# Cumulative sums of a decoder layer's state-space heads stored by head, so that a decay row is read in one piece

## The chip, the cores and the metric

The kernel runs on one core of one Trainium2 chip. What is measured is the device time of one execution in microseconds (us), from the first to the last instruction and what the runtime puts around them. Five engines work beside each other, each through its own instructions in order: TensorE (PE in the profile, its weight loads PEld), VectorE (DVE), ScalarE (ACT), GpSimd (POOL) and SyncE (SP), which only issues transfers. Transfers (DMAs) run on 16 engines of their own and are issued here from SP, ACT and POOL.

## What is computed

One decoder layer on 512 tokens of width 1024, in float32: a SwiGLU feed-forward part, a mixer, cross-attention to 256 memory tokens, a second feed-forward part and a norm. The mixer has two groups of heads that share an input and an output projection: eight differential-attention heads and 16 Mamba-2 (SSD) heads of width 64, in four groups. The change concerns the SSD heads. They work in chunks of 128 tokens:

```python
la_cum = jnp.cumsum(la, axis=2)                     # la = dt * a, per chunk and head
seg = la_cum[:, :, :, None] - la_cum[:, :, None, :]
decay = jnp.exp(jnp.where(causal[None, None, :, :, None, None], seg, -jnp.inf))
cb = jnp.einsum('bclgn,bcsgn->bclsg', cc, bc)
y_diag = jnp.einsum('bclsg,bclsgr,bcsgrp->bclgrp', cb, decay, xdt)
y_off = jnp.einsum('bclgn,bcgrpn,bclgr->bclgrp', cc, prev, jnp.exp(la_cum))
```

So each head needs, for its four chunks, the differences of the cumulative sums of all pairs of tokens in a chunk. For that, every partition (token s) needs the head's sums of all 512 tokens l in its row, and its own sum as a bias.

## The kernel before

**Precision and weights.** Most products are made of float32 split in two parts (`split_into`, L155 and L156: ACT rounds to the high part, DVE subtracts for the low part) and three matmuls. Weights come as 512 KB tiles `wr` by SP (`load_w`, L174; `raw_w`, L246) into six buffers, and are split into `wh` (ACT) and `wl` (DVE) before PE can use them. So behind each weight tile stand one ACT and one DVE instruction, in the order of those engines' streams.

**Order.** The work is written as generators. Dense ones (projections) run in a list; chains (attention heads, SSD groups, sums) are spawned with a due time and are taken between steps of the dense ones by a modelled PE clock. SP and POOL run in the order of the code; PE, DVE and ACT are put in order by the framework's scheduler. What each instruction waits for are semaphores; transfers of SP and ACT share eight of them (the lanes) in turn, so a transfer can't be issued until the previous one on its lane has landed.

**The cumulative sums.** After the `dt` projection (`steps_dense`, `pdt`), the chain `steps` makes `la` (128 tokens of a chunk on the partitions, chunk x head = 4 x 16 columns), and a matmul with a triangle of ones gives `cum` [128, 4, 16], at the time when the dense work is the attention's values (`by_token`, L356, with tiles `va`, `ve`, `vb`). `cum` is transposed on PE (`pct`, 64 rows = chunk x head, 128 tokens), copied by DVE to `ct_sb` (L727) and stored by POOL to `cum_d` in DRAM (L728), one row of 512 B for each chunk and head, chunks outermost.

**The decay rows.** `decays(g, j)` issues, on ACT's queue (L900), for two heads hd the load of the head's sums into all 128 partitions: 4 chunks x 128 tokens, 2 KB a partition, 256 KB in all. In `cum_d` a head's four chunks lie 16 rows apart, so that a partition's 2 KB come in four pieces of 512 B. The rows land in the tiles `gate` (j = 0) and `th` (j = 1), which the feed-forward parts use at other times. There are 16 such loads: four right behind the store, and four for each next group g + 1, issued in `group(g)`, two behind each of its two sets of `py` matmuls, when the tile is free again. ACT then makes of them the exponentials `e` (L964), the differences (L966) and the decays (L967), and DVE multiplies with `cbm` (L968).

**Others on the same queue.** The attention heads load their bias rows on ACT's queue too (`bias`, L757: 128 partitions x 2 KB, one piece each, eight times), for the softmax whose minimum `mn` DVE makes (L778). POOL and SP also copy and add up weight blocks in DRAM (`isum`, `wsum`, L1227 and L1231) for the last feed-forward part.

Of the kernel before, what the change touches and what calls it, by code (L numbers as in the profile page):

```python
# [11 lines left out]
F32 = mybir.dt.float32  # L12
# [5 lines left out]
P = 128  # L18
T = 512
# [81 lines left out]
def body(tc, a, dbg=None):  # L101
    nc = tc.nc
# [8 lines left out]
    dram = ctx.enter_context(tc.tile_pool(name="dram", bufs=1, space=bass.MemoryType.DRAM))  # L111
# [3 lines left out]
    def nm(s):  # L115
        uid[0] += 1
        return f"{s}_{uid[0]}"

    def s2(s, dt=F32, shape=(P, T)):
        if math.prod(shape[1:]) <= T // 2:  # L120
            return sp.tile(list(shape), dt, tag="s1", name=nm(s), bufs=NHALF)
        return sp.tile(list(shape), dt, tag="s2", name=nm(s))

    def s4(s):
        return sp.tile([P, 4, T // 2], F32, tag=s, name=nm(s), bufs=1)

    def small(s, n, bufs=None):
        return tiny.tile([P, n], F32, tag=s, name=nm(s), bufs=bufs)
# [4 lines left out]
    def aux(s, shape=(P, T)):  # L133
        return aux_p.tile(list(shape), F32, tag="aux", name=nm(s))

    def dump(name, t):
        if dbg and name in dbg:
            nc.sync.dma_start(dbg[name], t.bitcast(F32) if t.dtype == R32 else t)

    last, start, last_sum, recent, newest, newest_mm = [], [], [], [], [], []  # L140
    V, S, G = nc.vector, nc.scalar, nc.gpsimd
    od = Order()

    def mm(out, w, x, start, stop):
        od.t += (1 if w.dtype == R32 else 4) * (x.free_size() + 8) / 2400
        newest_mm[:] = [nc.tensor.matmul(out, w, x, start=start, stop=stop).ins]  # L146

    def transpose(out, x):
        od.t += 2 * (P + 8) / 2400
        nc.tensor.transpose(out, x, ident)  # L150
# [161 lines left out]
    def by_token(blocks, g, ps, done):  # L312
# [30 lines left out]
        kept = []  # L343
        w = weights("m1", 0)
        for i, (name, out, which, part) in enumerate(steps):
            (wh, wl), first = w, name in ("m1", "t")
            if i + 1 < len(steps):
                w = weights(steps[i + 1][0], steps[i + 1][3])
# [176 lines left out]
    def block_tiles(g, n):  # L525
        def steps(th, blocks, apart):
            b11 = [s2("g11" + p_, R32, (P, H)) for p_ in "hl"]
            split_into(*b11, th[:, 0])
            blocks["11"] = tuple(b11)
            yield apart  # L530
            for sums in sums_in_steps(*(th[:, i] for i in range(4)), pair=(th[:, 0:2], th[:, 1:3])):
                blocks |= sums or {}
                yield apart
            raw = split("g", th[:, 2:4].rearrange("p a b -> p (a b)"))
            lo, hi = slice(0, H), slice(H, T)
            blocks |= {"22": hl(raw, lo), "12": hl(raw, hi)}

        def made(th):
            g.append({})
            if len(g) < n:  # L540
                od.spawn(steps(th, g[-1], 2.9), 2.9)
            else:
                for _ in steps(th, g[-1], 0.0):
                    pass
        return made
# [52 lines left out]
    st_mix, h, h_sums = Stat(), [], []  # L598
# [59 lines left out]
    def bc_c(t):  # L658
        return t[:, None, :].to_broadcast([P, 4, 16])

    def flat(t):
        return t.rearrange("p a b -> p (a b)")

    def col64(s):
        return cp.tile([P, 4, 16], F32, name=s)

    cum, cdec, dend, dth = col64("cum"), col64("cdec"), col64("dend"), col64("dth")
    cum_d = dram.tile([64, P], F32, name="cum_d")

    def steps_dense():  # L670
        wdt = s2("wdt", shape=(P, KT, 16))
# [11 lines left out]
    def steps(pdt):  # L683
        dtf = s2("dtf", shape=(32, T))
        S.activation(dtf, pdt, AF.Copy)
        ii = s2("ii", shape=(32, 16))
        nc.gpsimd.dma_start(ii, a["ii"])
        hb = s2("hb", shape=(P, 2, 16))
        nc.gpsimd.dma_start(hb, a["hb"].partition_broadcast(P))
        yield 4.5  # L690
        pdk = aux("pdk", (P, 4, 16))
        for c in range(4):
            mm(pdk[:, c, :], dtf[:, c * P : (c + 1) * P], ii, True, True)
        dtr, dta, dtz, dte, dtp, la = (s2("dt", shape=(P, 4, 16)) for _ in range(6))
        V.tensor_tensor(dtr, pdk, bc_c(hb[:, 0]), ALU.add)

        S.activation(dta, dtr, AF.Abs)
        S.activation(dte, dta, AF.Exp, scale=-1.0)
        V.tensor_scalar(dtz, dte, 2.0, None, ALU.add)
        V.reciprocal(dtz, dtz)  # L700
        V.tensor_tensor(dtz, dtz, dte, ALU.mult)
        V.tensor_tensor(dte, dtz, dtz, ALU.mult)
        V.tensor_scalar(dtp, dte, 1.0 / 19, None, ALU.mult)
        for n in range(17, 2, -2):
            V.scalar_tensor_tensor(dtp, dtp, 1.0 / n, dte, ALU.add, ALU.mult)
        V.scalar_tensor_tensor(dtp, dtp, 1.0, dtz, ALU.add, ALU.mult)
        V.tensor_scalar(dtr, dtr, 0.0, None, ALU.max)
        V.scalar_tensor_tensor(dtr, dtp, 2.0, dtr, ALU.mult, ALU.add)
        dump("dt", dtr)
        ea = small("ea", 16, bufs=1)  # L710
        G.tensor_tensor(ea, euler[:, 0:1].to_broadcast([P, 16]), hb[:, 1], ALU.pow)
        V.scalar_tensor_tensor(la, dtr, -1.0, bc_c(ea), ALU.mult, ALU.mult)
        V.tensor_scalar(dth, dtr, 0.5, None, ALU.mult)
        yield 7.5
        pcum = aux("pcum", (P, 2, 64))
        mm(pcum[:, 0], tri, flat(la), True, True)
        mm(pcum[:, 1], ones, flat(la), True, True)
        V.tensor_copy(flat(cum), pcum[:, 0])
        V.tensor_tensor(flat(dend), pcum[:, 1], flat(cum), ALU.subtract)
        S.activation(flat(cdec), pcum[:, 1], AF.Exp)  # L720
        S.activation(dend, dend, AF.Exp)
        V.tensor_scalar(dend, dend, 0.5, None, ALU.mult)
        yield 1.5
        pct = aux("pct", (64, P))
        transpose(pct, flat(cum))
        ct_sb = s2("ct_sb", shape=(64, P))
        V.tensor_copy(ct_sb, pct)  # L727
        nc.gpsimd.dma_start(cum_d, ct_sb)  # L728
        for j in range(2):
            decays(0, j)  # L730
        dump("cum", cum)
# [162 lines left out]
    def decays(g, j):  # L894

        rows_of[g, j], both = [], s4(("gate", "th")[j])
        for hh in range(2):
            r = both[:, 2 * hh : 2 * hh + 2].rearrange("p a (b c) -> p (a b) c", c=P)
            hd = 4 * g + 2 * j + hh
            S.dma_start(r, bass.AP(cum_d.tensor, cum_d.offset + hd * P, [[0, P], [16 * P, 4], [1, P]]))  # L900
            rows_of[g, j].append(r)

    def group(g, bt, ct, xs, zs):
# [52 lines left out]
        for j in range(2):  # L956
# [21 lines left out]
            if g < 3:  # L978
                decays(g + 1, j)
# [497 lines left out]
```

## Time and profile before

| | |
|---|---|
| median of 3 runs | 1360.78 us (1359.14 to 1363.01) |
| profiled execution, its span | 1365.5 us (4.7 above the median; no other time of it is recorded) |
| PE busy | 1313.2 us, 96% |
| DVE, ACT, POOL busy | 998.0 (73%), 676.1 (50%), 117.2 (9%) |
| mean granted clock of TensorE | 0.982 |
| row loads (L900) | 16, of 256 KB each |
| first and last of them issued | at 432.7 and 799.7 us |

In the timeline a line gives start and duration in us, the engine (a q behind it: only the engine's sequencer is at work, as in issuing a transfer), line, operation, out<-in, how many, and in brackets the idle time of the engine before it and what ended it. In the list of waits a line gives who waited for whom, the sum in us, how often, and the longest. In a table by stage a line gives a stretch and its length, the busy time of PE, PEld, DVE, ACT and POOL with the number of instructions, the granted clock (1.00 is full), the busy share of the DMA engines and GB/s. Of one line's or tile's instructions the view gives the smallest, median and largest duration in ns, the first and last start, and the time from issue to landing. Names carry no buffer numbers, and a helper's line stands for all its callers.

### The profile page before, as it was taken

The page shows a single profiled execution, that of the slowest core. Times are in us where ns is not written, and L with a number is a line of the kernel's source. Part 1 is how long each engine was busy: PE and PEld are TensorE (multiplying, and loading weights), DVE is VectorE, ACT ScalarE, POOL GpSimd, SP SyncE. Part 2 cuts the span into 40 slices and gives each one's busy share as a digit, 9 for nine tenths or more (in the row PEclk, how much of TensorE's full clock was granted, in tenths as well). Part 3 has the DMA queues.
Part 4 walks back from the last instruction along what each step waited for, and adds up shares of the span by engine and source line. Part 5 has one row for each costly group of instructions (what it writes and reads, how often), then busy time and mean ns, then how long its engine had stood idle before and what let it go on. Part 6 is the DMA issues. An engine that isn't in the chain of part 4 may idle for free. (4 is left out here: it accounts for less than half of the span.)

```text
span 1365.5 us, 20091 instructions
## 1 busy us (share of the span) xinstructions
PE 1313.2 (96%) x7745; PEld 1138.7 (83%) x7745; DVE 998.0 (73%) x1565; ACT 676.1 (50%) x1134; POOL 117.2 (9%) x131
## 2 busy tenths in 40 slices
PE   9999999999977899998999998999999999999997
PEld 7898998899865577875788886888889989989995
DVE  6875778578885577656777777655587888977896
ACT  6441544245443466434646446434455555554564
POOL 0000011000010001110110220210001000000001
PEclk9999999999999899999999999999999999999998
DMA  7435586474464833665357747858057866666662
GB/s 264 123 109 131 147 207 220 105 199 142 141 163 123 243 106 78 156 184 165 74 125 208 176 111 252 246 161 223 33 155 180 233 211 187 178 194 183 181 205 93
DMA packets 75007, 225.85 MB, mean 165 GB/s; under 512 B 8520, under 2 KB 20272, under 8 KB 74560
## 3 DMA queue, kind: packets, MB, share of 16 engines
q1 hardware_dynamic: 52688, 175.47, 38.4%
q0 software_dynamic: 12480, 42.55, 17.4%
q10 hardware_dynamic: 9744, 6.56, 2.5%
q8 instruction: 61, 1.00, 0.3%
q14 instruction: 34, 0.28, 0.1%
HBM read 222.39 MB, written 50.91 MB: 200 GB/s over the span
## 5 line engine op out<-in xcount | busy, mean ns | idle before, releaser
L155 ACT ACTIVATE wh<-wr 128x1024 fp32r<-128x1024 f32 (+2 forms) x317 | 322.9, 1021 | 374.8 <-PE po L146 61.7
L156 DVE TENSOR_TENSOR wl<-wr,wh 128x1024 fp32r<-128x1024 f32 (+2 forms) x317 | 372.3, 1177 | 115.8 <-ACT wh L155 113.1
L146 PE MATMUL po<-gh,wh 128*128 128x512 f32 x176 | 68.8, 392 | 0.0
L146 PE MATMUL po<-gl,wh 128*128 128x512 f32 x176 | 68.5, 390 | 0.0
L146 PE MATMUL po<-gh,wl 128*128 128x512 f32 x176 | 68.4, 389 | 0.0
L240 PE MATMUL qa<-hmh,wl 128*128 128x256 f32 x216 | 61.2, 283 | 0.1
L240 PE MATMUL qa<-hml,wh 128*128 128x256 f32 x216 | 61.1, 283 | 0.0
L240 PE MATMUL qa<-hmh,wh 128*128 128x256 f32 x216 | 61.1, 283 | 0.0
L779 ACT ACTIVATE ec<-ec,mn 128x512 f32<-128x512 f32 (+3 forms) x64 | 35.5, 556 | 38.2 <-DVE mn L778 38.2
L146 PE MATMUL pxbc<-hnh,wh 128*128 128x512 f32 x128 | 52.3, 408 | 0.0
L146 PE MATMUL pxbc<-hnl,wh 128*128 128x512 f32 x128 | 50.3, 393 | 0.0
L146 PE MATMUL pxbc<-hnh,wl 128*128 128x512 f32 x128 | 50.2, 392 | 0.0
L584 DVE TENSOR_TENSOR upd<-po,row 128x512 f32<-128x512 f32 x24 | 16.6, 691 | 39.0 <-PE po L146 38.8
L240 PE MATMUL qb<-s31h,wh 128*128 128x256 f32 x152 | 43.2, 284 | 0.8 <-ACT u L299 0.8
L240 PE MATMUL qe<-s31h,wl 128*128 128x256 f32 x152 | 43.2, 284 | 0.5 <-DVE wl L156 0.5
L240 PE MATMUL qb<-s24h,wl 128*128 128x256 f32 x152 | 43.1, 284 | 0.5 <-DVE wl L156 0.5
L240 PE MATMUL qe<-s31h,wh 128*128 128x256 f32 x152 | 43.1, 283 | 0.2 <-DVE nlam L635 0.2
L240 PE MATMUL qb<-s24h,wh 128*128 128x256 f32 x152 | 43.0, 283 | 0.0
L240 PE MATMUL qe<-s24h,wh 128*128 128x256 f32 x152 | 43.0, 283 | 0.0
L240 PE MATMUL qb<-s31h,wl 128*128 128x256 f32 x152 | 43.0, 283 | 0.0
L240 PE MATMUL qe<-s24h,wl 128*128 128x256 f32 x152 | 43.0, 283 | 0.0
L240 PE MATMUL qb<-hmh,wh 128*128 128x256 f32 x152 | 43.0, 283 | 0.0
(490 smaller groups left out, 4105.0 us busy)
## 6 DMA issues: line engine op xcount, KB each, us to landing
wr<-in_f2q SPq DMA_DIRECT2D x44, 512.0 KB, 4.4
wr<-in_f1q SPq DMA_DIRECT2D x40, 512.0 KB, 4.3
isum<-in_f2q SPq DMA_DIRECT2D x22, 512.0 KB, 6.1
wr<-isum SPq DMA_DIRECT2D x22, 512.0 KB, 4.2
wsum<-in_f2b SPq DMA_DIRECT2D x20, 512.0 KB, 7.6
wr<-wsum SPq DMA_DIRECT2D x20, 512.0 KB, 4.4
wr<-in_f1q POOLq DMA_DIRECT2D x16, 512.0 KB, 5.8
wr<-in_f1o SPq DMA_DIRECT2D x16, 512.0 KB, 4.5
```

The source lines that it names most:

```text
L146: newest_mm[:] = [nc.tensor.matmul(out, w, x, start=start, stop=stop).ins]
L155: S.activation(hi, src, AF.Copy),
L156: V.tensor_tensor(lo, src, hi.bitcast(F32), ALU.subtract),
L240: newest_mm[:] = [nc.tensor.matmul(out, a_[:, wc], b_, start=first and f == 0 and kp == 0 and j == 0, stop=kp == n - 1 and j == 2, skip_gr ...
L584: V.tensor_tensor(upd, po, row4, ALU.mult)
L779: S.activation(ec[:, :n], ec[:, :n], AF.Exp, bias=mn, scale=-1.0, accum_out=sm[c][:, i : i + 1])
```

## The change

The sums are stored with the heads outermost: `cum_d` becomes [16, 512], a row of 2 KB for each head with its four chunks behind each other. The transpose must then give its 64 rows in the order head x chunk, so DVE first copies `cum` [token, chunk, head] to a new tile `ct_h` [token, head, chunk], and PE transposes that. The store writes the same 32 KB, from 64 partitions. A load reads one row of `cum_d`, broadcast to 128 partitions: the same 2 KB a partition, in one piece.

```diff
-    cum_d = dram.tile([64, P], F32, name="cum_d")
+    cum_d = dram.tile([16, T], F32, name="cum_d")
...
         pct = aux("pct", (64, P))
-        transpose(pct, flat(cum))
+        ct_h = s2("ct_h", shape=(P, 16, 4))
+        V.tensor_copy(ct_h, cum.rearrange("p c h -> p h c"))
+        transpose(pct, flat(ct_h))
         ct_sb = s2("ct_sb", shape=(64, P))
         V.tensor_copy(ct_sb, pct)
-        nc.gpsimd.dma_start(cum_d, ct_sb)
+        nc.gpsimd.dma_start(cum_d.rearrange("h (c t) -> (h c) t", t=P), ct_sb)
...
-            hd = 4 * g + 2 * j + hh
-            S.dma_start(r, bass.AP(cum_d.tensor, cum_d.offset + hd * P, [[0, P], [16 * P, 4], [1, P]]))
+            S.dma_start(r.rearrange("p a b -> p (a b)"), cum_d[4 * g + 2 * j + hh : 4 * g + 2 * j + hh + 1].to_broadcast([P, T]))
```

Lines behind L728 move down by two, and those from L901 on by one (L900 becomes L901). On DVE, where the sums are made, there stood (the numbers in the names are the buffers'):

```order
L718 COPY cum<-pcum_4243 128x64
L719 TENSOR_TENSOR dend<-pcum_4243,cum 128x64
L156 TENSOR_TENSOR wl_4288<-wr_4137,wh_4287 128x1024
L722 TENSOR_SCALAR dend<-dend 128x64
L727 COPY ct_sb_4263<-pct_4261 64x128
```

and now stand

```order
L718 COPY cum<-pcum_4243 128x64
L719 TENSOR_TENSOR dend<-pcum_4243,cum 128x64
L726 COPY ct_h_4262<-cum 128x64
L156 TENSOR_TENSOR wl_4290<-wr_4137,wh_4289 128x1024
L722 TENSOR_SCALAR dend<-dend 128x64
L729 COPY ct_sb_4265<-pct_4261 64x128
```

One copy has come in ahead of a weight split; the rest of DVE's order is the same to the end. On PE, at the same place, the transpose `pct` among the value matmuls stood before as

```order
L356 MATMUL vb_4098<-wh_4230,s24l_3981 128x512
L356 MATMUL vb_4098<-wl_4231,s24h_3980 128x512
L150 MATMUL pct_4261<-ident,cum 64x128
L356 MATMUL vb_4098<-wh_4230,s24h_4025 128x512
L356 MATMUL vb_4098<-wh_4230,s24l_4026 128x512
L356 MATMUL vb_4098<-wl_4231,s24h_4025 128x512
```

and stands now as

```order
L356 MATMUL vb_4098<-wh_4230,s24l_3981 128x512
L356 MATMUL vb_4098<-wl_4231,s24h_3980 128x512
L356 MATMUL vb_4098<-wh_4230,s24h_4025 128x512
L356 MATMUL vb_4098<-wh_4230,s24l_4026 128x512
L150 MATMUL pct_4261<-ident,ct_h_4262 64x128
L356 MATMUL vb_4098<-wl_4231,s24h_4025 128x512
```

It has moved behind two matmuls; nothing else on PE has changed place. On ACT, the four first loads and what stands behind them, before:

```order
L370 ACTIVATE u_743_4284<-vb_4099 128x512
L900 DMA gate_4266<-cum_d 128x4x128 x2
L900 DMA th_4269<-cum_d 128x4x128 x2
L155 ACTIVATE vh_4324<-p_731_4225 128x512
L155 ACTIVATE wh_4333<-wr_4112 128x1024
```

and now:

```order
L370 ACTIVATE u_744_4286<-vb_4099 128x512
L901 DMA gate_4268<-cum_d 128x512 x2
L901 DMA th_4271<-cum_d 128x512 x2
L155 ACTIVATE vh_4326<-p_731_4225 128x512
L155 ACTIVATE wh_4335<-wr_4112 128x1024
```

The order is the same, and the loads have become rows of 512 numbers. The orders of SP and POOL are unchanged.

## The prediction

> **What bounds the kernel now.** I read the page first, for the bound:
>
> ```profile
> span 1365.5 us, 20091 instructions
> PE 1313.2 (96%) x7745; PEld 1138.7 (83%) x7745; DVE 998.0 (73%) x1565; ACT 676.1 (50%) x1134; POOL 117.2 (9%) x131
> q10 hardware_dynamic: 9744, 6.56, 2.5%
> ```
>
> TensorE (PE) is busy for 96% of the span, so a change pays only where PE stands idle or runs at a lower clock. The queue that carries the decay rows, q10, takes 2.5% of the transfer engines: by volume it can't matter. By packets it is large for its 6.56 MB: 16 row loads of 128 x 4 pieces make 8192 of the 9744.
>
> Next came PE's waits over the whole run, for the places where it stands idle (us in total, times, longest):
>
> ```profile
> PE ve L356 <- ACT wh L155: 10.9, 1, 10.9
> PE ps L146 <- DVE mn L778: 7.6, 3, 5.7
> PE pdt L146 <- DVE ql L160: 7.6, 1, 7.6
> PE pm L146 <- ACT wh L155: 7.0, 2, 5.7
> PE pt L150 <- DVE mn L778: 1.6, 1, 1.6
> PE pq L146 <- ACT wh L155: 0.7, 1, 0.7
> PE pk L146 <- DVE wl L156: 0.5, 1, 0.5
> ```
>
> And the table by stage for the stretches at half clock (PE busy, PEld, DVE, ACT, POOL, then the granted clock):
>
> ```profile
> 440.20:450.30 10.10, 4.07 (x9) 2.80 (x10) 4.82 (x6) 4.59 (x6) 0.00 (x0) 0.50 0.85 131
> 474.30:481.10 6.80, 5.02 (x15) 3.95 (x16) 4.79 (x18) 4.40 (x13) 0.00 (x0) 0.50 0.61 228
> 593.80:597.10 3.30, 3.30 (x12) 2.79 (x10) 2.26 (x2) 0.55 (x1) 0.00 (x0) 0.50 0.75 187
> 624.50:631.30 6.80, 6.19 (x17) 4.62 (x17) 6.27 (x15) 4.03 (x9) 0.00 (x0) 0.50 0.60 181
> 825.90:832.60 6.70, 4.90 (x12) 3.77 (x13) 5.72 (x9) 4.84 (x9) 0.00 (x0) 0.50 0.90 264
> ```
>
> Each long wait is followed by such a stretch, in which PE's busy time counts double. The wait at pdt belongs to the projection that feeds the sums, so it is over before a row can be loaded; the others lie at the five places of this table, A to E in its order. The question is which of them the row loads cause.
>
> **Place A, the first four loads (433 to 451 us).** ScalarE (ACT) issues them itself, in order with its other work. Its timeline:
>
> ```profile
> 427.75 0.58 ACT L370 ACTIVATE u<-vb 128x512 f32<-128x512 f32 x1
> 432.71 1.10 ACTq L900 DMA_DIRECT2D gate<-cum_d  x2
> 433.85 10.66 ACTq L900 DMA_DIRECT2D th<-cum_d  x2
> 444.56 0.63 ACT L155 ACTIVATE vh<-p 128x512 fp32r<-128x512 f32 x1 [16.23 <-issue]
> 445.10 1.04 ACT L155 ACTIVATE wh<-wr 128x1024 fp32r<-128x1024 f32 x1
> ```
>
> PE's, and the store on POOL that the loads wait for:
>
> ```profile
> 446.19 0.79 PE L356 MATMUL ve<-wh,s24h 128*128 128x512 f32 x1 [10.90 <-ACT wh L155]
> 426.47 0.64 POOL L728 DMA_DIRECT2D cum_d<-ct_sb  x1 [25.92 <-DVE ct_sb L727]
> ```
>
> ACT is free at 428.3, is held until the store has landed (432.7), and is then held to 444.5 by the issues themselves, of which the second pair alone takes 10.66. Behind them in its queue stand vh and the weight split wh that PE waits for. The rows of the loads, and of the bias loads on the same queue, tell why:
>
> ```profile
> L900 ACTq DMA_DIRECT2D gate<-cum_d x8: 367/458/2368, 432.7 to 790.3; - x8
> L900 ACTq DMA_DIRECT2D th<-cum_d x8: 367/518/10101, 433.9 to 799.7; - x8
> DMA to landing us min/median/max: 7.5/11.8/29.8
> L757 ACTq DMA_DIRECT2D bias<-rel_z x8: 326/338/360, 401.1 to 664.6; - x8
> DMA to landing us min/median/max: 2.7/3.1/19.2
> ```
>
> A bias load is what a row load becomes: 128 partitions, 256 KB, one 2 KB piece each, on ACT's queue. Its issue never took over 360 ns; a row load's took up to 10101. So the 10 us go with the number of pieces: four loads put 2048 into one queue, and the fourth has to wait until it has drained. After the change the four put 512 there, as many as the first load alone does now, and the first pair (1024) is issued in 1.10.
>
> What the change adds here is one strided copy on DVE and a later transpose; the nearest row for the copy is
>
> ```profile
> 424.25 0.23 DVE L718 COPY cum<-pcum 128x64 f32<-128x64 f32 x1 [0.65 <-PE pcum L146]
> ```
>
> Queued behind it are the DVE split wl, ct_sb and the store, so the store lands some 0.23 late, at 432.9. It delays ACT by that much; for PE, matmuls at hand cover it. If that cover is gone it costs 0.2 to 0.5. Of the moved transpose (one matmul, two places later) nothing remains beside it. Four issues take 1.4 (at 338 ns) to 2.2 (at the first pair's 0.55); I take 1.7, so ACT goes on at 434.6 instead of 444.56. PE follows 1.63 behind (446.19 - 444.56), at 436.3: of the 10.9 idle 1.0 is left, a gain of 9.9. The 4.07 busy at half clock become 2.0, a gain of 2.0. Behind the first matmuls DVE's split is next late, since vl and wl follow ACT's: 0.5 back. Together 11.4.
>
> Whether the 1.5 us left idle still lowers the clock is open. The nearest row is place C, where waits of about 1.4 and 0.7 were followed by the stretch from 593.80 at 0.50, at a price of half of its 3.30. I charge half of that, 0.8: A gains 10.6. The ends: 9 with the whole lowered clock (1.6) and the slower issues, 12 without DVE's 0.5.
> The Trainium skill (TensorE: Matmul & The Clock Gate, "HAM oscillation — how this bites in real kernels") says that only idle gaps over about 3.4 us lower the clock; by that rule A would be 11.4. The trace disagrees: no gap before 593.80 was so long.
>
> **Place B (470 to 481).** SyncE (SP) shares completion lanes with ACT's queue, so its prefetch waits for the row loads to land:
>
> ```profile
> SPq L1227 <- DMA gate<-cum_d: 15.5, 1, 15.5
> 449.05 2.91 SPq L174 DMA_DIRECT2D wr<-in_wk  x1
> 468.50 1.06 ACT L155 ACTIVATE wh<-wr 128x1024 fp32r<-128x1024 f32 x1 [10.30 <-DMA wr<-in_wk]
> ```
>
> The key weights are issued right behind that wait and land only at 468.4. ACT's and DVE's splits of them hold up the softmax work behind, and PE waits at pk (0.5), ps (7.6 less the 5.7 of place D) and pt (1.6): 4.0. The 5.02 at half clock cost 2.5. The lane comes free when the first load has landed, which by the 15.5 is some 16 us after its issue now; with a quarter of the pieces I estimate 4 to 6, so the weights are issued about 10 earlier and have fewer pieces to compete with; PE, some 11 earlier, needs them at about 458 (468.5 less 10.6). Even at the old 19.4 from issue (449.05) to use they would be there at about 458. I count all 6.5; the ends are 0 and 6.5.
>
> **Places C and D (584 to 631).** The next loads, on ACT, and what waits for them:
>
> ```profile
> 584.30 2.78 ACTq L900 DMA_DIRECT2D gate<-cum_d  x2
> 587.13 1.29 ACT L964 ACTIVATE e<-th 64x512 f32<-64x512 f32 x2 [6.17 <-DVE y L992]
> 591.32 0.61 ACT L155 ACTIVATE wh<-wr 128x512 fp32r<-128x512 f32 x1
> 591.99 0.50 PE L146 MATMUL pm<-yah,wh 128*128 128x512 f32 x1 [1.36 <-ACT wh L155]
> 598.43 1.22 ACTq L900 DMA_DIRECT2D th<-cum_d  x2
> 605.00 0.34 ACTq L757 DMA_DIRECT2D bias<-rel_z  x1
> 624.35 0.69 DVE L778 CUSTOM_DVE_ANT_0 ec<-ps,bias 128x512 f32<-128x512 f32 x1 [10.15 <-DMA bias<-rel_z]
> ```
>
> C: the exponentials e (587.13) start as soon as the two issues are done, and wh (591.32) shows no idle time before it. So 2.78 becoming 0.7 brings wh 2.1 earlier and covers the 1.4. The wait at pq (0.7) and 1.7 of half clock go only if DVE's splits also come up: 3.7 at most, 0 at least, I take 2.5.
> D: the bias of the next head stands in ACT's queue behind 1024 row pieces and lands 19.2 after its issue; DVE is idle for 10.15 and PE for 5.7. With 256 pieces ahead, the 605.00 issue should land by 610, at the median 3.1 by 608, while DVE is ready only at 614. So all 5.7 go, and half of 6.19: 8.8. The lower end is 5.7.
>
> **Place E and the later loads** stay. At E, ACT waits for DVE and then has its queue full:
>
> ```profile
> 820.36 1.29 ACT L155 ACTIVATE ysh<-y 128x512 fp32r<-128x512 f32 x2 [2.69 <-DVE y L1009]
> 827.04 0.61 ACT L155 ACTIVATE wh<-wr 128x512 fp32r<-128x512 f32 x1
> ```
>
> The split that PE wants (5.7 at pm) starts 6.7 later and has no idle time before it; what ACT waited for is y, not a row load. The loads around 734 and 790 hold up no matmul; their speed is worth nothing. In the built program PE now also waits on the loads' lanes ahead of 16 py matmuls; ACT has read those rows long before, so I charge 0.4 for instructions alone.
>
> **Sum.** 10.6 + 6.5 + 2.5 + 8.8 - 0.4 = 28.0 us against the profiled span: 1365.5 - 28.0 = 1337.5. That execution is 4.7 above the median of the three runs, 1360.78, of which I take the same 28.0: **1332.8**.
>
> **Rivals.**
> 1. The key weights become what is late. They land at 468 as now, for the transfers ahead of them rather than for the lane. For: the 10.30 in the row of 468.50. Against: they were issued at 449 only because of the lane. Then PE arrives early and waits, A and B are worth nothing, C and D bring 11.3: 1349.5. Chance 0.09.
> 2. Bytes, not pieces, set the pace: the same 4 MB are read, 128 partitions from one row as before. Then ACT's issue and the landings stay: 1361.0. For: q10's median of 11.8 would fit a slow shared source. Against: bias loads of the same bytes take 3.1 and 338 ns. Chance 0.06. The Trainium skill (DMA: Bandwidth & Descriptors, "Specifications") speaks for it: it calls 512 B enough for line rate; the issue of 10101 ns is not explained by that.
> 3. Slower: SP, released early, puts its DRAM copies of 512 KB ahead of the key weights while POOL's are under way. It decides once the weights land after 480, 12 past today's 468, when C and D are used up; each further us costs one. Landing at 486 gives 1366. It needs some 45 us from issue to landing, where 19 is the worst seen at B. Chance 0.02.
>
> **How the numbers follow.** The forecast has 0.83. All terms at their upper ends (12, 6.5, 3.7, 8.8) give 31.0 and 1329.8, and the runs scatter by some 2 below: 1327. At the lower ends, with half of B (9, 3.2, 0, 5.7), 17.9 give 1342.9; 3 more for a part given back later: 1346. The rivals lie outside, with 0.17. Faster by over 0.3% (4 us, about what a measurement of this kernel can tell from none): 0.92; within: 0.06; slower: 0.02.
>
> **What would show it.** Right: row loads issued in under 0.6 us each, landing in 3 to 8; PE going on near 436 to 437; PE's waits at ve about 1, at ps and pt near nothing, and 6 us at pm left; two or three half-clock stretches fewer. Wrong: an ACT issue of several us, a bias wait of DVE near 600, a wait for in_wk, or PE waits past 860 that are not there now.

## The result and the profile after

| | before | after |
|---|---|---|
| median, us (4 runs each on one chip) | 1359.96 (1356.42 to 1363.01) | 1339.29 (1336.95 to 1341.09) |
| profiled execution, its span, us | 1365.5 | 1335.1 (timed as 1336.95) |

The ratio of the times is 0.9842 [0.9811, 0.9874]: 20.7 us faster, where 28.0 had been forecast and 1332.8 named. From profile to profile it is 30.4. The two figures differ by the two executions that were profiled. The new one is the fastest of four, 2.3 under its median. Its time is 1.8 above its span; with the same 1.8 the profiled execution before took 1367.3, 7.3 above the median of its kernel. 30.4 - 7.3 - 2.3 = 20.8.

The head of the page after, to set beside that of before:

```profile
span 1335.1 us, 20107 instructions
PE 1302.0 (98%) x7745; PEld 1131.7 (85%) x7745; DVE 997.6 (75%) x1566; ACT 676.2 (51%) x1134; POOL 116.5 (9%) x131
q10 hardware_dynamic: 3600, 6.56, 1.5%
```

The packets of q10 went from 9744 to 3600, and their time from 2.5% to 1.5%. PE's waits after the change (us in total, times, longest), of the places that the prediction speaks of:

```profile
PE pdt L146 <- DVE ql L160: 7.5, 1, 7.5
PE pm L146 <- ACT wh L155: 6.1, 2, 5.7
PE ve L356 <- ACT wh L155: 1.8, 1, 1.8
PE pq L146 <- ACT wh L155: 0.7, 1, 0.7
PE ve L356 <- DVE wl L156: 0.5, 1, 0.5
```

Gone are the 10.9 at ve, the ps, pt and pk; the 5.7 at pm (place E) and the wait at pdt stay. The table by stage after, behind place A and at place E (length, PE busy, PEld, DVE, ACT, POOL, granted clock):

```profile
436.60:446.00 9.40, 8.85 (x38) 7.03 (x39) 8.35 (x9) 6.50 (x9) 0.00 (x0) 1.00 1.06 275
795.00:801.50 6.50, 3.55 (x8) 2.70 (x9) 5.48 (x9) 5.99 (x13) 0.00 (x0) 0.50 0.37 109
```

Behind A the clock is no longer lowered at all; at E it still is. ACT at place A after:

```profile
427.36 0.58 ACT L370 ACTIVATE u<-vb 128x512 f32<-128x512 f32 x1
432.71 1.01 ACTq L901 DMA_DIRECT2D gate<-cum_d  x2
433.77 1.18 ACTq L901 DMA_DIRECT2D th<-cum_d  x2
434.99 0.63 ACT L155 ACTIVATE vh<-p 128x512 fp32r<-128x512 f32 x1 [7.05 <-issue]
435.53 1.04 ACT L155 ACTIVATE wh<-wr 128x1024 fp32r<-128x1024 f32 x1
```

The second pair is issued in 1.18 us instead of 10.66, and ACT goes on 9.6 earlier. Of its 7.05 some 4.8 are the wait for the store to land (427.94 to 432.71), the rest the issues. PE there:

```profile
436.62 0.50 PE L356 MATMUL ve<-wh,s24h 128*128 128x512 f32 x1 [1.76 <-ACT wh L155]
437.88 0.50 PE L356 MATMUL ve<-wl,s24h 128*128 128x512 f32 x1 [0.53 <-DVE wl L156]
```

PE goes on at 436.62 instead of 446.19, and the 0.53 is the wait for DVE's split. The row loads by line, and the softmax step that waited 10.15 us for its bias at place D:

```profile
L901 ACTq DMA_DIRECT2D gate<-cum_d x8: 326/386/1528, 432.7 to 760.5; - x8
L901 ACTq DMA_DIRECT2D th<-cum_d x8: 326/444/767, 433.8 to 769.9; - x8
DMA to landing us min/median/max: 3.4/4.9/13.5
595.58 0.69 DVE L780 CUSTOM_DVE_ANT_0 ec<-ps,bias 128x512 f32<-128x512 f32 x1 [2.17 <-PE ps L146]
```

The bias wait is gone: that step now waits for PE. Landings went from a median of 11.8 us to 4.9, but at worst still take 13.5. The key weights, whose late landing was rival 1, are issued at 442.3 and land at 448.7 (449.05 and 468.4 before).

**The time by stretch.** PE's order is nearly the same in all kernels here, so the time between the starts of two given matmuls can be set side by side, kernel by kernel. A runs from the first `va` matmul to the 25th (408.16 to 451.22 in the trace before), B on to the 31st `ps` (491.63), C from the first `py` (583.16) to the 97th `ps` (615.36), D on to the 131st `ps` (642.79). Between B and C lie 91.5 to 91.6 us in every kernel. The lower part of the table is that of the experiments.

| kernel | row loads | A | B | C | D | median, us |
|---|---|---|---|---|---|---|
| before | 4 pieces, 8 KB apart | 43.1 | 40.4 | 32.2 | 27.4 | 1359.96 |
| after | 1 piece | 32.5 | 33.0 | 29.7 | 18.5 | 1339.29 |
| e1 | as before | 43.6 | 37.3 | 32.1 | 26.8 | (one run) |
| e9 | 4 pieces, 16 KB apart | 42.9 | 33.8 | 32.0 | 25.9 | 1358.23 |
| e2 | 4 pieces, 640 B apart | 39.8 | 33.1 | 30.6 | 18.5 | 1345.74 |
| e6 | 4 pieces, 1 KB apart | 39.9 | 33.1 | 29.8 | 18.5 | 1345.25 |
| e5 | 4 pieces, 10 KB apart | 39.8 | 33.1 | 32.5 | 18.4 | 1345.21 |
| e10 | 4 pieces, 12 KB apart | 40.2 | 33.0 | 30.0 | 18.5 | 1345.62 |
| e3 | first four 1 piece, later as before | 36.2 | 33.4 | 30.3 | 28.1 | 1348.89 |
| e4 | first four as before, later 1 piece | 40.5 | 34.3 | 31.9 | 18.5 | 1348.26 |
| e7 | as before, first four spread out | 29.6 | 43.9 | 29.6 | 27.2 | 1354.52 |
| e11 | 1 piece (after) | 33.6 | 33.0 | 29.8 | 18.5 | 1340.81 |
| e8 | 1 piece, first four later | 29.7 | 33.3 | 29.7 | 18.5 | 1336.36 |
| e12 | as e8 | 29.6 | 33.0 | 32.2 | 18.4 | 1336.26 |

From profile to profile the change brings 10.6 at A, 7.4 at B, 2.5 at C and 8.9 at D, 29.4 of the 30.4; the rest lies ahead of A (0.4) and between D and the last matmul (0.6). Each row is one execution, while the median is that of all runs of the kernel.

### The profile page after: what moved, and what is told of

Read it like the earlier page. It is cut to its first block, busy times and chain, and to the rows that moved or that the text cites. A ratio compares the mean times of both kernels' runs of the same rounds, so it can differ in the third digit from the quotient of the medians.

```text
span 1335.1 us, 20107 instructions
## 1 busy us (share of the span) xinstructions
PE 1302.0 (98%) x7745; PEld 1131.7 (85%) x7745; DVE 997.6 (75%) x1566; ACT 676.2 (51%) x1134; POOL 116.5 (9%) x131
## 5 line engine op out<-in xcount | busy, mean ns | idle before, releaser
L781 ACT ACTIVATE ec<-ec,mn 128x512 f32<-128x512 f32 (+3 forms) x64 | 35.5, 556 | 30.6 <-DVE mn L780 30.6
L240 PE MATMUL qb<-s31h,wh 128*128 128x256 f32 x152 | 43.1, 284 | 1.1 <-ACT u L299 1.1
L240 PE MATMUL qb<-s24h,wl 128*128 128x256 f32 x152 | 43.1, 284 | 0.5 <-DVE wl L156 0.5
L240 PE MATMUL qe<-s31h,wh 128*128 128x256 f32 x152 | 43.1, 284 | 0.0
L240 PE MATMUL qb<-hml,wh 128*128 128x256 f32 x152 | 43.0, 283 | 0.0
```

The source lines that it names most:

```text
L240: newest_mm[:] = [nc.tensor.matmul(out, a_[:, wc], b_, start=first and f == 0 and kp == 0 and j == 0, stop=kp == n - 1 and j == 2, skip_gr ...
L781: S.activation(ec[:, :n], ec[:, :n], AF.Exp, bias=mn, scale=-1.0, accum_out=sm[c][:, i : i + 1])
```

## The experiments

The theory on record is that of the number of pieces: 2048 of them hold up ACT's issue, and land slowly. Its rival: not how many they are but where they lie in DRAM. A second question is why the median moved less than the profiles. All kernels compute the whole result. The ratios are to the kernel before on the same chip, whose median there was 1359.66 (e1 to e4), 1360.6 (e5 to e8) and 1362.17 us (e9 to e12); they are worked out from the single runs, so they differ a little from the quotient of the medians.

### e1: the kernel before, once more

No edit.

> The kernel before, unchanged, profiled once more. Between the two profiles the change saved 30.4 us, between the medians of the times 20.7. Theory (the waits of before vary from run to run, and its first profile caught a long one): at least one of the four places lost (10.9 us at ve, 4.0 at pk, ps and pt, 2.1 at pm and pq, 5.7 at ps) is shorter by several us here, and the span is near 1358 instead of 1365.5. Rival (the changed kernel gives some of it back in most executions, and its profile caught a good one): the four waits are as before within 1 us, the span is 1364 to 1367.

It took 1362.63 us, span 1360.9. Neither expectation holds as a whole: only B is shorter than in the first profile, by 3.1, and the span is not near 1358. Its table by stage there (length, PE busy, ..., granted clock):

```profile
473.00:480.50 7.50, 6.40 (x27) 5.00 (x28) 6.34 (x22) 4.29 (x12) 0.00 (x0) 0.77 0.45 153
```

A mean of 0.77, where before had 6.8 us at 0.50: the lowered clock lasts half as long here, in the same kernel. So B's length is no constant of the kernel. This run stood above its median too; 41 runs of before lie between 1353.56 and 1367.49, so that the first profile (1367.3 by the 1.8) stands at their slow end.

### e2: by head, but in four pieces

```diff
-    cum_d = dram.tile([16, T], F32, name="cum_d")
+    cum_d = dram.tile([64, 160], F32, name="cum_d")
...
-        nc.gpsimd.dma_start(cum_d.rearrange("h (c t) -> (h c) t", t=P), ct_sb)
+        nc.gpsimd.dma_start(cum_d[:, :P], ct_sb)
...
-            S.dma_start(r.rearrange("p a b -> p (a b)"), cum_d[4 * g + 2 * j + hh : 4 * g + 2 * j + hh + 1].to_broadcast([P, T]))
+            hd = 4 * g + 2 * j + hh
+            S.dma_start(r, bass.AP(cum_d.tensor, cum_d.offset + hd * 4 * 160, [[0, P], [160, 4], [1, P]]))
```

> The changed kernel, but each head's four rows of 512 B lie 640 B apart, so that a partition's row comes in four pieces again; order of the heads, copy, transpose and number of loads are those of the change. Theory (the number of pieces): q10 has 9744 packets again, an issue of 8 to 11 us at the fourth load, and the time is that of before: ratio 0.997 to 1.003. Rival (it is the place of the rows in DRAM, by head and near each other): the time is that of the change, ratio 0.984.

1345.74 us, 0.9904 [0.9884, 0.9924]: between the two, and neither forecast came. The wait at ve is 7.4 and the longest issue 6766 ns, which speaks for the pieces; but B and D are those of the changed kernel with 9744 packets, which the number of pieces doesn't explain.

### e3 and e4: the first four loads and the later twelve, each alone

Both layouts are stored (`cum_c` as before, one more transpose, copy and store); in e3 only the loads of group 0 read the new one, in e4 only those of the later groups.

```diff
...
-            S.dma_start(r.rearrange("p a b -> p (a b)"), cum_d[4 * g + 2 * j + hh : 4 * g + 2 * j + hh + 1].to_broadcast([P, T]))
+            hd = 4 * g + 2 * j + hh
+            if g == 0:
+                S.dma_start(r.rearrange("p a b -> p (a b)"), cum_d[hd : hd + 1].to_broadcast([P, T]))
+            else:
+                S.dma_start(r, bass.AP(cum_c.tensor, cum_c.offset + hd * P, [[0, P], [16 * P, 4], [1, P]]))
```

> Both layouts are stored, the one by head first; the first four loads read one piece, the later twelve four pieces. Theory: places A and B are mended and C and D are not: waits at ve near 2, none at pt, bias again late at about 600; ratio 0.987 to 0.992. Rival (the issue stall of the first four alone makes the gain, the later loads nothing): ratio 0.984.

> Both layouts are stored, the one by chunk first; the first four loads read four pieces, the later twelve one. Theory: C and D are mended, A and B are not: an issue of 8 to 11 us at the fourth load, wait at ve 10 to 11; no wait for the bias; ratio 0.992 to 0.996. Rival (the first four alone): ratio 1.00.

e3: 1348.89, 0.9928 [0.9905, 0.9952] (its profile is of its slowest run, 1353.01); e4: 1348.26, 0.9924 [0.9901, 0.9946]. The gains, 10.8 and 11.4, add up to 22.2, about the whole change (20.7). The ratio of e3 lies just outside its range, and its wait at ve is 3.3 instead of near 2. In e4 the fourth issue took 7.2 us and the wait at ve was 8.1, both less than expected. D belongs to the later loads alone (28.1 in e3, 18.5 in e4). A belongs mostly to the first four (36.2 and 40.5). B doesn't follow them so plainly: 34.3 in e4, where they landed in up to 26.0 us.

### e5: the order of before, rows padded

```diff
-    cum_d = dram.tile([64, P], F32, name="cum_d")
+    cum_d = dram.tile([64, 160], F32, name="cum_d")
...
-        nc.gpsimd.dma_start(cum_d, ct_sb)
+        nc.gpsimd.dma_start(cum_d[:, :P], ct_sb)
...
-            S.dma_start(r, bass.AP(cum_d.tensor, cum_d.offset + hd * P, [[0, P], [16 * P, 4], [1, P]]))
+            S.dma_start(r, bass.AP(cum_d.tensor, cum_d.offset + hd * 160, [[0, P], [16 * 160, 4], [1, P]]))
```

> The kernel before, chunks outermost, but with 640 B from row to row instead of 512, so that a head's four pieces lie 10 KB apart instead of 8 KB. The run with four pieces 640 B apart was 14 us faster than before with the same number of pieces. Theory (near pieces are read quickly, pieces many KB apart slowly): as before, last of the first four landing 26 to 31 us after its issue, ratio 0.997 to 1.003. Rival (a distance that is a power of two is what is slow): like the run with pieces 640 B apart, landing 12 to 14, ratio 0.990.

1345.21 us, 0.9885 [0.9864, 0.9905]. No sorting by head, no copy, the same 9744 packets, only 128 B of padding behind each row, and 15.4 of the 20.7 us are there. The theory on record for this run (pieces many KB apart are slow) is refuted by it. The loads of e5, by line:

```profile
L900 ACTq DMA_DIRECT2D gate<-cum_d x8: 367/458/2673, 431.8 to 770.3; - x8
L900 ACTq DMA_DIRECT2D th<-cum_d x8: 366/520/6856, 433.0 to 779.7; - x8
DMA to landing us min/median/max: 3.2/5.7/12.6
```

The landings are near those of single pieces (4.9 in the median, 13.5 at worst, after the change), while the longest issue is still 6856 ns. So where the pieces lie sets the landing, and how many they are still costs an issue of this length.

### e6: by head, pieces 1 KB apart

As e2 with 256 instead of 160.

> The change with four pieces again, a head's rows 1024 B apart, so that its four pieces span 3.5 KB. Theory (near pieces are read quickly): like the run with 640 B, ratio 0.990, an issue of 6 to 8 us, landings of the first four 12 to 14. Rival (the distance that is a power of two): slow landings, 20 us and more, ratio 0.995 to 1.003.

1345.25 us, 0.9885 [0.9863, 0.9907]: as e5 and e2. A distance of 1 KB, a power of two, is not slow.

### e9 and e10: by chunk, pieces 16 KB and 12 KB apart

As e5 with 256 (e9) and 192 (e10) instead of 160.

> The kernel before, chunks outermost, rows 1024 B apart, so that a head's four pieces lie 16 KB apart. With 10 KB they were fast, with 8 KB slow. Theory (a distance that is a multiple of 8 KB is slow): as before, last of the first four landing 26 to 31 us after its issue, ratio 0.997 to 1.003. Rival (rows packed close to each other, 512 B from head to head, are what is slow, and any gap mends it): landing 12 to 14, ratio 0.987 to 0.991.

> The same with rows 768 B apart, four pieces 12 KB apart. Theory (multiples of 8 KB): fast, ratio 0.987 to 0.991, landing 12 to 14. Rival (any multiple of 4 KB is slow): landing over 20, ratio 0.993 to 1.003. Rival (gaps between rows): fast as well, told apart by the run with 16 KB.

e9: 1358.23, 0.9988 [0.9966, 1.001]; e10: 1345.62, 0.9889 [0.9857, 0.992]. Loads by line in e9, and D's softmax step on DVE:

```profile
L900 ACTq DMA_DIRECT2D gate<-cum_d x8: 366/450/2117, 433.1 to 781.9; - x8
L900 ACTq DMA_DIRECT2D th<-cum_d x8: 366/523/9210, 434.2 to 791.3; - x8
DMA to landing us min/median/max: 7.7/11.9/25.2
617.35 0.69 DVE L778 CUSTOM_DVE_ANT_0 ec<-ps,bias 128x512 f32<-128x512 f32 x1 [9.91 <-DMA bias<-rel_z]
```

and the loads in e10:

```profile
L900 ACTq DMA_DIRECT2D gate<-cum_d x8: 366/450/1726, 434.0 to 770.1; - x8
L900 ACTq DMA_DIRECT2D th<-cum_d x8: 366/520/6971, 434.9 to 779.5; - x8
DMA to landing us min/median/max: 4.6/7.0/14.9
```

e9 stores the same 64 rows, 1 KB apart, as e6; only the order differs, and with it the distance of a partition's pieces. At 16 KB the slow landing and the bias wait are back, at 12 KB they are not. So padding by itself cures nothing: 8 and 16 KB are slow, 640 B, 1, 10 and 12 KB are not. Both ratios came as the theory of multiples of 8 KB had it.

### e7: the layout of before, the first four loads spread out

Each of them is put behind a later weight split on ACT (`newest` holds the last one), 10 us of PE's modelled time apart.

```diff
+            newest[:] = recent[:1]
...
-            decays(0, j)
+            for hh in range(2):
+                yield 10.0
+                with behind(list(newest)):
+                    decays(0, j, (hh,))
...
```

The part left out lets `decays` issue one head's load at a time.

> The kernel before with its old layout, but the first four loads stand in ACT's queue one by one behind four weight splits of the following 25 us. Theory (ACT is held by the pieces still in its queue, and places A and B come from that and from the late lanes): no issue over 3 us, the wait at ve falls from 11 to under 2 and the half clock behind it goes: 8 to 12 us gained at A; B may stay, since the landings are as slow as before; C and D stay. Ratio 0.991 to 0.994. Rival (the landings alone count, not the issue): the wait moves to another place on PE, ratio 0.998 to 1.003.

1354.52 us, 0.9946 [0.9926, 0.9965]. A is 29.6: no wait at ve, and none of these issues over 423 ns. But B grows to 43.9, where PE now waits:

```profile
462.21 0.47 PE L150 MATMUL pt<-ident,ec 128*128 128x128 f32 x1 [3.30 <-DVE mn L782]
473.19 0.55 PE L150 MATMUL pt<-ident,ec 128*128 128x128 f32 x3 [0.90 <-DVE ec L794]
```

13.5 of A are won, more than the 8 to 12 expected, and 3.5 of them given back at B (6.6 when e1's B is taken); D stays at 27.2. With the issue stall gone and the slow landing left, 6.1 us of the median are gained, and the ratio lies just above its range.

### e8, e11 and e12: the change with its first four loads later, and the change again

```diff
+            newest[:] = recent[:1]
...
-        for j in range(2):
-            decays(0, j)
+        yield 12.0
+        with behind(list(newest)):
+            for j in range(2):
+                decays(0, j)
```

> The changed kernel with the first four loads behind a later weight split on ACT, so that ACT needn't wait for the store to land while PE waits for a split. Theory: the waits of 1.8 and 0.5 at ve go; 2 to 3 us faster than the change, ratio to before 0.982 against 0.984 (1336 to 1338 us). Rival (what ACT waits for there is hidden, or comes back as a wait elsewhere): equal to the change within 1 us.

> The changed kernel once more, beside the version with later first loads. Theory (the changed kernel scatters little, since no transfer is waited for any more but the weights at ve): 1337 to 1341 us, ratio 0.983 to 0.986, waits at ve of 1.5 to 2.5 and no wait for a bias. Rival (its first profile was a lucky one): waits at pk, ps or pt of over 1 us in this profile.

> The changed kernel with the first four loads behind a later weight split, on the same chip as the changed kernel. Theory: 2 to 3 us faster than that one, ratio to before 0.981 to 0.983. Rival: the 2.9 between the two came from different chips, and they agree within 1 us.

e8: 1336.36, 0.9814 [0.9791, 0.9837]. On one chip e11: 1340.81, 0.9852 [0.9827, 0.9877], and e12: 1336.26, 0.9819 [0.9793, 0.9845]. Moving the loads behind the weight split takes another 4.5 us off the change (2 to 3 were expected), whose runs it doesn't overlap with (1333.88 to 1338.7 and 1339.69 to 1341.74), and is the best version here. What they still cost at A shows in e11, where a clock lowered to about half follows the two short waits of PE (its timeline, and its table by stage right behind):

```profile
437.97 0.50 PE L356 MATMUL ve<-wh,s24h 128*128 128x512 f32 x1 [1.30 <-ACT wh L155]
439.23 0.50 PE L356 MATMUL ve<-wl,s24h 128*128 128x512 f32 x1 [0.53 <-DVE wl L156]
439.70:443.10 3.40, 3.40 (x10) 2.63 (x9) 2.94 (x4) 1.26 (x3) 0.00 (x0) 0.51 1.06 233
```

A is 33.6 there and 29.6 in e12, whose profile has neither wait nor lowered clock at A. In e12 place C shows what it showed before the change:

```profile
571.52 0.50 PE L146 MATMUL pm<-yah,wh 128*128 128x512 f32 x1 [1.36 <-ACT wh L155]
572.99 0.50 PE L146 MATMUL pq<-hnh,wh 128*128 128x512 f32 x1 [0.74 <-ACT wh L155]
574.00:577.40 3.40, 3.40 (x19) 2.95 (x19) 2.15 (x3) 0.00 (x0) 0.00 (x0) 0.50 0.85 246
```

So C's 2.5 us can be lost with single pieces, and with four pieces at the old distance they can be saved (e7: 29.6). The first wait, at pm, follows the issue of the second `gate` load of this place: in all 14 traces it is 1.00 to 1.06 us shorter than that issue. But that issue took 1.30 to 2.67 us with four pieces and 1.49 to 2.42 with one, so it does not go with their number. What makes it long was not tried.

Nor does the wait alone decide whether a lowered clock follows: after 1.36 and 0.74 it does in e12, after 1.34 and 0.73 it doesn't in e2. In every trace here all changes of the granted clock lie whole steps of 3.413 us apart (before: the stretches A to E begin 10, 35, 9 and 59 steps after each other), and the steps lie differently against the kernel in each execution. Here are the steps in which the waits fall, first C in e12 and in e2 with the step behind it, then A in e11 and two steps of A after the change (PE's busy time stands behind the length):

```profile
570.62:574.03 3.41, 1.77 (x7) 1.16 (x7) 2.78 (x5) 3.27 (x6) 0.00 (x0) 1.00 0.00 0
580.62:584.03 3.41, 1.93 (x7) 1.33 (x8) 2.79 (x5) 3.11 (x5) 0.00 (x0) 1.00 0.00 0
584.03:587.45 3.42, 3.42 (x30) 2.83 (x30) 3.08 (x5) 0.00 (x0) 0.00 (x0) 1.00 0.95 293
436.33:439.74 3.41, 1.58 (x6) 0.76 (x5) 2.49 (x4) 3.40 (x5) 0.46 (x1) 1.00 0.95 256
432.98:436.40 3.42, 1.88 (x9) 1.22 (x7) 0.69 (x1) 1.41 (x2) 1.50 (x2) 1.00 0.94 322
436.40:439.81 3.41, 2.66 (x10) 1.91 (x11) 3.21 (x4) 3.19 (x5) 0.00 (x0) 1.00 0.98 201
```

With PE busy for 1.77 and 1.58 of a step, the next one is at half clock; with 1.88, 1.93 and 2.66 it isn't. Over all 14 traces (20 to 1320 us) the 53 full-clock steps that a lowered one follows have PE busy for at most 0.52 of their length, and all others for more, but for three at 0.45 to 0.51; the ends of matmuls are modelled, so the border is rough. After the change the idle 1.76 and 0.53 at A fall into two steps, in e11 the 1.30 and 0.53 into one.

## Why the prediction was right, and where it was not

**The places.** It named four places and left E; the profiles agree: 10.6 at A (10.6 forecast), 7.4 at B (6.5), 2.5 at C (2.5), 8.9 at D (8.8), nothing lost elsewhere. The 2.5 at C are luck. They were to come from two issues that shrink from 2.78 to 0.7; they took 1.86 (0.33 and 1.53), and 2.75 in e12, where C is 32.2 as before. None of the rivals came: the key weights landed in time (448.7), the issue shrank, SP's copies did no harm.

**The step that failed**, though the time came out within the range, is the last of the sum: "That execution is 4.7 above the median of the three runs, 1360.78, of which I take the same 28.0." The profiled execution was a slow one of its kernel (7.3 above the median, not 4.7, since 1.8 lie outside the span), and part of what it lost at B was its own. The mis-sized term is B: 40.4 us in that profile, but 37.3 in e1 and 33.8 in e9, which lands its pieces about as slowly, against 33.0 without slow pieces. "The 5.02 at half clock cost 2.5" was true of one execution. Between two profiles nearer to their medians, e1 and e11, the gains are 9.9 at A, 4.2 at B, 2.3 at C and 8.3 at D, less 2.3 that e11 lost ahead of A, where its clock was lowered for 10.2 us and that of e1 for 6.8: 22.4 in all, with the spans (1360.9 - 1338.4 = 22.5), near the 20.7 of the medians. What B loses goes with the landing of the first key weights: they landed 17.2, 14.5, 11.3 and 11.2 us after B's start in before, e1, e4 and e9, and B took 40.4, 37.3, 34.3 and 33.8; after the change 8.4 and 33.0. (In e7 it is the later key tiles that land late.) ACT's first split of them, in e1, e9 and e4:

```profile
465.51 1.06 ACT L155 ACTIVATE wh<-wr 128x1024 fp32r<-128x1024 f32 x1 [7.66 <-DMA wr<-in_wk]
462.48 1.06 ACT L155 ACTIVATE wh<-wr 128x1024 fp32r<-128x1024 f32 x1 [4.32 <-DMA wr<-in_wk]
460.60 1.06 ACT L155 ACTIVATE wh<-wr 128x1024 fp32r<-128x1024 f32 x1 [4.44 <-DMA wr<-in_wk]
```

They were issued at 447.8 to 449.1 in all four, but took 19.4 us to land in before, 17.1 in e1, 14.4 in e9 and 12.7 in e4. Why two executions of one kernel differ by 2.3 there, and why e4 and e9 need less with slow row loads ahead, was not settled.

**The reason was half right.** "So the 10 us go with the number of pieces" holds for the issue: with pieces that land quickly, the longest issue of 2048 pieces is still 5.7 to 7.0 us (e2, e5, e6, e10) and A is 39.8 to 40.2 against 32.5 with one piece. That is 7.3 of the 10.6. The other 3.3 appear at 8 and 16 KB in before, e1 and e9 (an issue of 9.2 to 10.9 us), but hardly in e4, which at 8 KB has an issue of 7.2 and an A of 40.5; so they are not shown to be the distance's. And the fourth load does not wait "until it has drained": by the packet records 525 of the 2112 packets of the four loads had been moved in before when its issue ended, 452 to 584 in e1, e2, e4, e5, e9 and e10, and 181 in e6. At B and D the number of pieces does nothing: 33.0 to 33.1 and 18.4 to 18.5 with four as with one. There the slow landing of pieces 8 KB apart did it. The argument from the bias loads ("A bias load is what a row load becomes") changed number and place at once and could not tell them apart, and rival 2 weighed only bytes against pieces. That the sum came out near for the two profiles all the same is luck in this respect: the change does away with both causes at once. In medians the distance is worth 14 to 17 us (e2, e5, e6, e10) and the number another 4.8 on one chip (e10 and e11). The number was varied only where the pieces land quickly; with slow landing e7, which takes the issue out of the way, gives 6.1.

**The landing at A** was estimated at 4 to 6 us. The issue of one piece being fast, the transfers still took up to 13.5, and SP's wait became 8.7 instead of 15.5 (SP's waits after):

```profile
SPq L1228 <- DMA gate<-cum_d: 8.7, 1, 8.7
```

It cost nothing, as the prediction had argued for even the old 19.4 us: PE has no wait for the key weights left.

**The details of A.** ACT went on at 434.99 (434.6 forecast), PE at 436.62 (436.3), and the 0.53 for DVE's split is the 0.5 that was charged. Whether the short idle time lowers the clock was left open at half its price, 0.8. It goes either way, with how the idle time falls into the steps of 3.413 us: not in the profile after (1.76 and 0.53 of idle), but in e11 (1.30 and 0.53). At C the 0.7 at pq stayed, as it was to do unless DVE's splits came up, yet the lowered clock went without that: the 1.36 had become 0.48, and PE was busy for more of the step. The Trainium skill (TensorE: Matmul & The Clock Gate, "HAM oscillation — how this bites in real kernels") asks for a gap of over some 3.4 us; the rows of e11 and e12 show lowered clocks behind gaps of 1.30 and 0.53, and of 1.36 and 0.74, so it is no bound to rely on.

**E and the extra waits.** The 0.4 charged for instructions doesn't show; the part from D's end to the last matmul is 0.6 shorter, while over all kernels it lies between 710.6 and 713.3.

## What to carry to other kernels

A load that is small in bytes can hold up an engine's stream by its issue and hold up its neighbours in the queue by its landing; measure the two apart, since here the landing went with where the pieces lie and most of the long issue with how many they are. Try padded rows first, at more than one pitch: 128 B behind each row brought three quarters of the gain here, 512 B brought nothing (e9). And before a sum is carried from one profiled execution to the median, ask where that execution stands among the runs, and which of its lowered-clock stretches a second profile shows again. A short wait may cost only itself in one execution, and half of a lowered-clock step of 3.41 us more in the next.

## What the runs showed of the hardware

- The same 512 B pieces, 128 partitions reading the same four, land slowly when the four lie 8 or 16 KB apart (medians of 11.8 and 11.9 us, at worst 29.8 and 25.2) and quickly at 640 B, 1, 10 or 12 KB (5.4 to 7.0, at worst 11.6 to 14.9). The Trainium skill (DMA: Bandwidth & Descriptors, "Latency and other measured facts") tells of rows that lie large powers of two apart, with figures from 512 KiB on, and of padding as the cure; here 8 KB is slow and 1 KB is not. Whether it is the same effect, and whether other multiples of 8 KB are slow, was not tried.
- ACT's issue of the fourth load behind 1536 pieces took 5.7 to 10.9 us in the profiles, with 7.2 in e4 where landings were slow: it does not simply follow the landing. It ended when some 450 to 590 of the 2112 packets had been moved (181 in e6).
- Of four loads of one piece, the last was issued in 0.69 us after the change but in 2.94 in e3, so single pieces are not wholly free either. In e8 and e12 such loads landed in up to 19.9 and 18.5 us, without a wait of PE at ve or in B.
- The granted clock changed only on steps of 3.413 us, and it fell to half behind steps in which PE was busy for about half or less (at most 0.52 in 53 cases of 14 traces; three such steps, at 0.45 to 0.51, were not followed by it).
